# ConvFFN input product of a hybrid decoder: pairs of weight tiles multiplied by seven block products

## Chip, cores and metric

One core of a Trainium2 chip runs the whole program. The metric is the device time of one execution in microseconds (us). A profile of one execution is read beside the times.

## What is computed

Two layers of a decoder trunk run for 512 prompt tokens and 8 sample tokens, all in fp32. The part that matters is the last third of a layer, the ConvFFN, with d_model 1024 and d_ff 2816:

```python
def conv_ffn(h, buf, p):
    a, g = split_cols(h @ p['w_ffn_in'], (D_FF, D_FF))
    a, new_buf = causal_dwconv(a, buf, p['ffn_conv_w'], p['ffn_conv_b'])   # 3 taps along tokens
    return (jax.nn.silu(a) * g) @ p['w_ffn_out'], new_buf
# in decoder_layer, for each of the 2 layers
f, new_buf_ffn = conv_ffn(rmsnorm(x, p['norm_ffn_pre']), buf_ffn, p)
x = x + rmsnorm(f, p['norm_ffn_post'])
```

## The kernel before

Activations lie with features on the 128 partitions and tokens along the free dimension: a tile is `[128, 2, 260]`, two halves of 256 prompt and 4 sample tokens. A model vector is 8 such tiles (the k blocks), the hidden vector of the ConvFFN 22 (`NFF`). The kernel is written in a framework that puts each engine's instructions in an order of its own, by readiness and program order, with all semaphores; each engine then runs its queue in that order. Buffers come from pools: `ck` (56 buffers of a tile's size, function `C`), `ld` (8 buffers for loads, `LD`), weights (`wr` raw with 3 buffers, `wh` and `wl` with 4 each), PSUM (`PD` of two banks, twice; `PS` of one bank, four times).

A product keeps fp32 accuracy in one of two ways. In most, weights and activations are cut into a high part in fp32r (`wh`, a ScalarE cast, line 169) and a low part (`wl`, a VectorE subtraction, line 111), and three matmuls per k block are summed: high by high, high by low, low by high (`mm3`, line 195). `dense` does this for one 128-column tile of weights: 8 k blocks, 3 products, 2 halves. Directly after a norm, where the activations are late, `after_norm` instead multiplies uncut fp32 tiles ("exact products" below, line 407; the profile shows two matmul records for each), while `late`, a generator, finishes the residual sum, its square sums (`Sum`, `Rms`) and the cuts `sp` of x in between. In both cases 1/rms (`r`) is applied to the result when it leaves PSUM.

The ConvFFN's first product has 22 pairs of tiles, an `a` tile `wf[j]` and a gate tile `wf[NFF + j]`. The first three tiles (a 0, gate 0, a 1) are exact products in `after_norm`, the other 41 are `dense`. `ffn_a` scales the a tile by 1/rms into `pb` and calls `ffn_conv` (three taps, tanh: one ScalarE step, two VectorE steps at line 114, tanh on ScalarE, one VectorE step); `ffn_g` scales the gate tile into `gg`, `ffn_mul` multiplies on VectorE. `ffn_sample` does the sample tokens for 6 to 8 tiles at once. The results `us` are cut into `uss` (8 of them inside the loop) for the second product, `w_ffn_out`, done by `post`, whose steps alternate with the next layer's `memory_kv`. Weight loads go through SP's queue, small loads and stores through GpSimd's. GpSimd has two small instructions per pair (a memset, line 1489; a copy, line 1503). Elsewhere it multiplies whole tiles: in the mixer at lines 1142 and 296, and near the program's end in `bulk` at lines 335 and 338. VectorE's helpers are `tt` (line 111, two tensors) and `stt` (line 114, two tensors and a scalar).

## Time and profile before

| what | value |
|---|---|
| median of 3 runs | 3201.56 us (3200.24 to 3203.86) |
| profiled execution, its own time | 3205.31 us |
| its span, first to last instruction | 3203.5 us |
| mean granted TensorE clock | 0.996 |
| matmul records | 25878 |

In the rows, PE is TensorE's matmul, PEld its weight load, DVE VectorE, ACT ScalarE, POOL GpSimd, SP the engine that issues most loads. L195 is line 195. Times are from the span's start. `out<-in` names the tiles; xN counts instructions; a bracket is the idle time before and what ended it. Instructions of an engine overlap a little in the records, so the distance between two starts is the better price of one.

### The profile page before, as it was taken

The numbers are of one execution on the slowest core, as the hardware profiler recorded it, in microseconds if no ns is written. First come the engines' busy times: TensorE is split into PE (matmuls) and PEld (weight loads), VectorE is DVE, ScalarE is ACT, GpSimd is POOL, SyncE is SP. The second block draws the span as 40 slices with busy tenths as digits, with TensorE's granted clock in tenths as the row PEclk, the third lists the DMA queues.
The fourth block names the chain that finished last, engine by engine and source line by source line (L and its number), as shares of the span: only waits on it lengthen the run. The fifth ranks groups of instructions, "written<-read, shape, count | busy, mean of one in ns | idle before, by whom it ended". The sixth has DMA issues, their size and how long they took to land. (4 is left out here: it accounts for less than half of the span.)

```text
span 3203.5 us, 64089 instructions
## 1 busy us (share of the span) xinstructions
PE 3160.6 (99%) x25878; PEld 3020.2 (94%) x25878; DVE 1949.0 (61%) x3773; ACT 1454.4 (45%) x3348; POOL 423.9 (13%) x762
## 2 busy tenths in 40 slices
PE   8999999999999999999999999999999999999998
PEld 7989999999999879999999899999999998899998
DVE  6665686777553537665286666777775436376643
ACT  5343566666433434333243445676673233433331
POOL 1100222122300101000020011222223001010001
PEclk9999999999999999999999999999999999999999
DMA  7322444444643553223263234444455336432231
GB/s 258 122 83 100 140 166 150 146 162 160 215 139 107 186 172 127 96 96 109 88 228 110 80 103 162 158 140 160 153 183 197 123 109 213 147 129 96 94 96 64
DMA packets 192168, 445.83 MB, mean 139 GB/s; under 512 B 26416, under 2 KB 78656, under 8 KB 191872
## 3 DMA queue, kind: packets, MB, share of 16 engines
q1 hardware_dynamic: 162736, 353.63, 33.0%
q0 software_dynamic: 27840, 86.01, 7.9%
q8 instruction: 203, 3.33, 0.4%
q10 hardware_dynamic: 1296, 2.11, 0.2%
q14 instruction: 93, 0.76, 0.1%
HBM read 377.81 MB, written 63.83 MB: 138 GB/s over the span
## 5 line engine op out<-in xcount | busy, mean ns | idle before, releaser
L169 ACT CAST wh<-wr 128x1024 fp32r<-128x1024 f32 (+1 forms) x484 | 503.4, 1041 | 1139.6 <-PE pd L195 763.9
L111 DVE TENSOR_TENSOR wl<-wr,wh 128x1024 fp32r<-128x1024 f32 (+1 forms) x484 | 591.4, 1223 | 523.3 <-ACT wh L169 514.4
L195 PE MATMUL pd<-xih,wh 128*128 128x260 f32 x3488 | 716.8, 287 | 3.2 <-ACT dd L108 3.2
L195 PE MATMUL pd<-xih,wl 128*128 128x260 f32 x3488 | 702.6, 283 | 0.0
L195 PE MATMUL pd<-xil,wh 128*128 128x260 f32 x3488 | 702.1, 283 | 0.0
L195 PEld LDWEIGHTS pd<-xih,wh 128*128 128x128 f32 x3488 | 536.8, 189 | 25.3 <-issue 19.2
L195 PEld LDWEIGHTS pd<-xih,wl 128*128 128x128 f32 x3488 | 537.7, 188 | 0.1
L195 PEld LDWEIGHTS pd<-xil,wh 128*128 128x128 f32 x3488 | 537.6, 189 | 0.1
L195 PE MATMUL pd<-sph,wh 128*128 128x260 f32 x1472 | 298.0, 284 | 0.0
L195 PE MATMUL pd<-spl,wh 128*128 128x260 f32 x1472 | 296.4, 283 | 0.0
L195 PE MATMUL pd<-sph,wl 128*128 128x260 f32 x1472 | 295.8, 282 | 0.0
L195 PEld LDWEIGHTS pd<-sph,wh 128*128 128x128 f32 x1472 | 226.8, 188 | 2.9 <-issue 2.7
L195 PEld LDWEIGHTS pd<-spl,wh 128*128 128x128 f32 x1472 | 227.9, 189 | 0.0
L195 PEld LDWEIGHTS pd<-sph,wl 128*128 128x128 f32 x1472 | 226.7, 188 | 0.1
L114 DVE SCALAR_TENSOR_TENSOR cv<-pb,hw,cv 128x512 f32<-128x512 f32 x192 | 143.6, 748 | 5.5 <-ACT cv L108 0.7
L251 POOL TENSOR_TENSOR ny<-nms,mhalf 128x3 f32<-128x3 f32 (+2 forms) x26 | 39.2, 1506 | 787.6 <-DVE nms L250 787.6
L195 PE MATMUL pd<-uh,wh 128*128 128x260 f32 x616 | 124.1, 283 | 0.0
L195 PE MATMUL pd<-uh,wl 128*128 128x260 f32 x616 | 123.9, 282 | 0.0
L195 PE MATMUL pd<-ul,wh 128*128 128x260 f32 x616 | 123.6, 282 | 0.0
L108 ACT ACTIVATE th<-cv 128x512 f32<-128x512 f32 x64 | 40.5, 633 | 154.4 <-DVE cv L114 133.0
L296 DVE TENSOR_TENSOR acc<-acc,sq 128x260 f32<-128x260 f32 (+1 forms) x126 | 61.8, 513 | 76.6 <-ACT sq L108 75.2
L195 PEld LDWEIGHTS pd<-ul,wh 128*128 128x128 f32 x616 | 95.1, 188 | 0.0
(425 smaller groups left out, 6052.1 us busy)
## 6 DMA issues: line engine op xcount, KB each, us to landing
wr<-in_w_in SPq DMA_DIRECT2D x218, 512.0 KB
wr<-in_w_ffn_in SPq DMA_DIRECT2D x88, 512.0 KB
hs<-in_ssm SPq DMA_DIRECT2D x64, 256.0 KB
csb<-csd SPq DMA_DIRECT2D x64, 256.0 KB
out_s_ssm<-hs POOLq DMA_DIRECT2D x64, 256.0 KB, 2.8
mem_k<-in_mem_k SPq DMA_DIRECT2D x64, 256.0 KB
wr<-in_w_ssm_out SPq DMA_DIRECT2D x32, 512.0 KB
mem_v<-in_mem_v SPq DMA_DIRECT2D x64, 256.0 KB
```

Of the source, the lines that this page charges most:

```text
L108: return A.activation(out, in_, f, **kw)
L111: return V.tensor_tensor(out=out, in0=a, in1=b, op=op)
L114: return V.scalar_tensor_tensor(out=out, in0=a, scalar=s, in1=b, op0=op0, op1=op1)
L169: A.copy(h[:, :nk], raw[:, :nk])
L195: PE.matmul(ps, a[:, k], b[:, hf], start=(first and k == 0 and i == 0), stop=(last and k == nk - 1 and i == 2))
L251: G.tensor_tensor(out=y, in0=ms, in1=mhalf[:, 0:n], op=ALU.pow)
L296: (E or V).tensor_tensor(out=AV(self.acc, h), in0=AV(self.acc, h), in1=AV(sq, h), op=ALU.add)
```

## The change

The kernel multiplies the a tile and the gate tile of a pair together, for pairs 2 to 21. The pair is taken as a 2 by 2 block matrix (two tiles by two halves of the 8 k blocks), the activations as another (two halves of k by two halves of the tokens), and the four block results come from seven block products with sums of operands and results (Strassen's form, Winograd's variant) in place of eight. The weights' sums s1, s2 and two in-place differences are made on GpSimd, and each combination (`a1`, `c1` to `c4`) is cut into high and low parts by ScalarE and VectorE (`cut`). The activations' combinations (`b11`, `b21`, `b22`, `t1` to `t4`) are made once per layer in `late_seven`, from x scaled by 1/rms and the norm's gain, so no scaling is left when a result leaves PSUM. Partial results are copied from PSUM (`p`, `q`) and added to later ones. Pairs 0 and 1, four tiles, are exact products in `after_norm4`. The product with the gate moves from VectorE to GpSimd, the small sample copies to ScalarE, all cuts of `us` and the start of the next `memory_kv` behind the loop. The pool `ld` is merged into `ck` (64 buffers).

```diff
...
 PAST = 2048
 THETA = 500000.0
 NEG = -1e30
-NCK = 56
+NCK = 64
 NM1 = 18
-NLD = 8
...
         ckpool = es.enter_context(tc.tile_pool(name="ck", bufs=NCK))
-        ldpool = es.enter_context(tc.tile_pool(name="ld", bufs=NLD))
...
         def LD(s, shape, dt=F32):
-            return ldpool.tile(list(shape), dt, tag="ld", name=nm(s))
+            return ckpool.tile(list(shape), dt, tag="ck", name=nm(s))
...
-        def post(w, xs_, gain, src, keep, nwin, nxt=None, final=False):
+        def post(w, xs_, gain, src, keep, nwin, nxt=None, final=False, seven=False):
...
             r2 = C("r2") if nxt else None
-            sp = [(C("sph", dt=F32R), C("spl", dt=F32R)) for _ in range(8)] if nxt else None
+            if seven:
+                sp = {}
+            else:
+                sp = [(C("sph", dt=F32R), C("spl", dt=F32R)) for _ in range(8)] if nxt else None
...
+            def late_seven():
+                squares(0)
+                rm[1].spread(r)
+                bulk(1)
+                yield
+                rm2[0] = Rms(sq2.acc, D, 0)
+                squares(1)
+                yield
+                rm2[0].spread(r2)
+                yield
+                xn = [C("xn") for _ in range(8)]
+                def scaled(hf):
+                    for m in range(8):
+                        stt(xn[m][:, hf], mg[m][:, hf], nxt(m), r2[:, hf], ALU.mult, ALU.mult)
+                def pair(a, b):
+                    h, l = C("sxh", dt=F32R), C("sxl", dt=F32R)
+                    for i, v in enumerate((a, b)):
+                        split_to(h[:, i], l[:, i], v)
+                    return [(h[:, i], l[:, i]) for i in range(2)]
+                def put(na, nb, ps_):
+                    sp[na] = [v[0] for v in ps_]
+                    sp[nb] = [v[1] for v in ps_]
+                scaled(0)
+                put("b11", "b21", [pair(xn[k][:, 0], xn[k + 4][:, 0]) for k in range(4)])
+                yield
+                rm2[1] = Rms(sq2.acc, D, 1, pd=rm2[0].pd)
+                yield
+                rm2[1].spread(r2)
+                yield
+                scaled(1)
+                ta, tb = [], []
+                for k in range(4):
+                    a, b = C("ta"), C("tb")
+                    tt(a[:, 0], xn[k][:, 1], xn[k][:, 0], ALU.subtract)
+                    tt(a[:, 1], xn[k + 4][:, 1], a[:, 0], ALU.subtract)
+                    G.tensor_tensor(out=b[:, 0], in0=xn[k + 4][:, 1], in1=xn[k][:, 1], op=ALU.subtract)
+                    G.tensor_tensor(out=b[:, 1], in0=xn[k + 4][:, 0], in1=a[:, 1], op=ALU.subtract)
+                    ta.append(a)
+                    tb.append(b)
+                put("t1", "t2", [pair(a[:, 0], a[:, 1]) for a in ta])
+                v = [pair(xn[k + 4][:, 1], xn[k + 5][:, 1]) for k in (0, 2)]
+                sp["b22"] = v[0] + v[1]
+                put("t3", "t4", [pair(b[:, 0], b[:, 1]) for b in tb])
+                store()
+                yield
...
             if nxt:
-                return mg, sp, r2, late()
+                return mg, sp, r2, late_seven() if seven else late()
...
+        def after_norm4(aps, x, gain, late, evac):
+            steps = ((1, 2), (1, 7), (2, 4), (3, 1), (4, 4), (5, 1))
+            ws = [load_wg(ap, 8, gain) for ap in aps]
+            out = {}
+            pd = None
+            for j in range(8):
+                hf, i = divmod(j, 4)
+                if j in (4, 5):
+                    pd = pd or PD()
+                    ps = pd[:, j % 2]
+                else:
+                    ps = PS()
+                for k in range(8):
+                    PE.matmul(ps[:, :HALF], ws[i][:, k], x[k][:, hf], start=(k == 0), stop=(k == 7))
+                    if (j, k) in steps:
+                        next(late)
+                    if (j, k) in ((2, 4), (5, 1)):
+                        for i2 in range(4):
+                            if (i2, 0 if j == 2 else 1) in out:
+                                evac(i2, out.pop((i2, 0 if j == 2 else 1)), 0 if j == 2 else 1)
+                out[i, hf] = ps
+                if j == 3:
+                    for i2 in range(4):
+                        if (i2, 0) in out:
+                            evac(i2, out.pop((i2, 0)), 0)
+                if j == 5:
+                    next(late)
+            for (i2, hf), ps in out.items():
+                evac(i2, ps, hf)
+        def seven_products(ap0, ap1, X):
+            w0, w1 = [wpool.tile([P, 8, P], F32, tag="wr", name=nm("wr"), bufs=3) for _ in range(2)]
+            nc.sync.dma_start(out=w0, in_=ap0)
+            nc.sync.dma_start(out=w1, in_=ap1)
+            def W():
+                return [wpool.tile([P, 8, P], F32R, tag=t, name=nm(t)) for t in ("wh", "wl")]
+            def cut(t, x, o, n):
+                h, l = [v[:, o:o + n] for v in t]
+                A.copy(h, x)
+                tt(l, x, h.bitcast(F32), ALU.subtract)
+                return h, l
+            def sub(out, a, b, op=ALU.subtract):
+                G.tensor_tensor(out=out, in0=a, in1=b, op=op)
+            s1, s2 = C("s1", (P, 4, P)), C("s2", (P, 4, P))
+            sub(s1, w1[:, 0:4], w1[:, 4:8], ALU.add)
+            sub(s2, s1, w0[:, 0:4])
+            t = W()
+            a1 = cut(t, w0, 0, 8)
+            sub(w0[:, 4:8], w0[:, 4:8], s2)
+            sub(w1[:, 0:4], w0[:, 0:4], w1[:, 0:4])
+            t12 = W()
+            c1 = cut(t12, s1, 0, 4)
+            c2 = cut(t12, s2, 4, 4)
+            c4 = cut(W(), w0[:, 4:8], 0, 4)
+            c3 = cut(W(), w1, 0, 8)
+            def mm(ps, w, k0, xs, first):
+                h, l = w
+                for k in range(4):
+                    xh, xl = xs[k]
+                    for i, (a, b) in enumerate(((h, xh), (h, xl), (l, xh))):
+                        PE.matmul(ps, a[:, k0 + k], b, start=(first and k == 0 and i == 0), stop=(k == 3 and i == 2),
+                                  skip_group_check=True)
+            pd = PD()
+            de, be = pd[:, 0, :HALF], pd[:, 1, :HALF]
+            al, ga = PS()[:, :HALF], PS()[:, :HALF]
+            p, q = C("pp"), C("pq")
+            mm(be, a1, 0, X["b11"], True)
+            A.copy(p[:, 0], be)
+            mm(al, a1, 4, X["b21"], True)
+            yield 0, 0, al, p[:, 0]
+            mm(de, c1, 0, X["t1"], True)
+            A.copy(q[:, 0], de)
+            mm(be, c2, 0, X["t2"], False)
+            A.copy(p[:, 1], be)
+            mm(de, c4, 0, X["b22"], False)
+            yield 0, 1, de, p[:, 1]
+            mm(be, c3, 0, X["t3"], False)
+            A.copy(q[:, 1], be)
+            yield 1, 1, be, q[:, 0]
+            mm(ga, c3, 4, X["t4"], True)
+            yield 1, 0, ga, q[:, 1]
...
             x, xss, r, late = drain(post(I["w_xo"][L], oxs, lambda m: pc("xpost", m), x_src, keep, 3,
-                                         lambda m: pc("ffnpre", m)))
+                                         lambda m: pc("ffnpre", m), seven=True))
...
                 tt(QV(gth[j], hf), PV(r, hf), PV(ps, hf), ALU.mult)
                 tt(S8(g_s[:, j], hf), SV(r, hf), SV(ps, hf), ALU.mult)
-                if hf is None and j > 1:
-                    ffn_mul(j)
             def ffn_mul(j):
                 tt(PV(us[j]), PV(us[j]), QV(gth[j]), ALU.mult)
...
             wf = I["w_ffn_in"][L]
             def first(i, ps, hf):
-                (ffn_a, ffn_g, ffn_a)[i]((0, 0, 1)[i], ps, hf)
-            after_norm([wf[0], wf[NFF], wf[1]], x, lambda k: pc("ffnpre", k), late, first)
-            for j in range(1, NFF):
-                if j > 1:
-                    ffn_a(j, dense(wf[j], xss), None)
-                ps = dense(wf[NFF + j], xss)
-                ffn_g(j, ps, None)
-                if j == 1:
-                    for i in range(2):
-                        ffn_conv(i)
-                        ffn_mul(i)
+                (ffn_a, ffn_g)[i % 2](i // 2, ps, hf)
+            after_norm4([wf[0], wf[NFF], wf[1], wf[NFF + 1]], x, lambda k: pc("ffnpre", k), late, first)
+            for j in range(2):
+                ffn_conv(j)
+                ffn_mul(j)
+            for j in range(2, NFF):
+                pb = apb[j] = C("pb", (P, 520))
+                gg = C("gg")
+                G.memset(pb[:, 0:2], 0.0)
+                for i, hf, ps, part in seven_products(wf[j], wf[NFF + j], xss):
+                    if i == 0:
+                        o = 2 + 256 * hf
+                        tt(pb[:, o:o + HALF], ps, part, ALU.add)
+                        A.copy(fnew[:, j, 4 * hf:4 * hf + 4], pb[:, o + 256:o + HALF])
+                        if hf:
+                            ffn_conv(j)
+                    else:
+                        tt(gg[:, hf], ps, part, ALU.add)
+                A.copy(S8(g_s[:, j]), SV(gg))
+                G.tensor_tensor(out=PV(us[j]), in0=PV(us[j]), in1=PV(gg), op=ALU.mult)
                 if j == 8:
                     ffn_sample(0, 8)
-                if 9 <= j < 17:
-                    uss[j - 9] = split(us[j - 9], "u")
                 if j == 16:
                     ffn_sample(8, 16)
-                if j == 18 and L < DEPTH - 1:
-                    mem_dram = mem_scratch()
-                    mkv = memory_kv(L + 1, *mem_dram)
-                    next(mkv)
             ffn_sample(16, 22)
-            for j in range(8, NFF):
+            for j in range(NFF):
                 uss[j] = split(us[j], "u")
+            if L < DEPTH - 1:
+                mem_dram = mem_scratch()
+                mkv = memory_kv(L + 1, *mem_dram)
+                next(mkv)
             G.dma_start(out=O["p_ffn_conv"][L], in_=psf)
             G.dma_start(out=O["s_ffn_conv"][L, :, :, 1], in_=fnew)
             last = L == DEPTH - 1
```

## Rows read from the trace of the kernel before

**Rows 1.** The page, busy time by engine: us, share of the span, instructions.

```profile
PE 3160.6 (99%) x25878; PEld 3020.2 (94%) x25878; DVE 1949.0 (61%) x3773; ACT 1454.4 (45%) x3348; POOL 423.9 (13%) x762
```

**Rows 2.** Busy time by stretch: from:to, length, engines in turn, granted clock, DMA.

```profile
1210.00:1237.10 27.10, 25.56 (x133) 21.70 (x132) 22.18 (x55) 15.19 (x32) 9.23 (x13) 1.00 0.44 143
1237.10:1472.90 235.80, 235.80 (x1970) 235.76 (x1969) 156.63 (x280) 82.65 (x109) 9.19 (x44) 1.00 0.32 106
1472.90:1596.00 123.10, 123.10 (x1028) 123.10 (x1027) 39.59 (x54) 37.65 (x53) 1.64 (x1) 1.00 0.30 91
2823.90:3059.50 235.60, 235.60 (x1965) 235.60 (x1965) 151.39 (x269) 77.25 (x96) 9.19 (x44) 1.00 0.30 101
```

**Rows 3.** The chain that ended last, in order of time: start, us, what.

```profile
2823.89 346.66 PE pd L195 x2892
```

**Rows 4.** Groups by line in 1237.1:1472.9, TensorE: count | busy us, mean ns | idle.

```profile
L195 PE MATMUL pd<-sph,wh 128*128 128x260 f32 x656 | 132.0, 283 | 0.0
```

**Rows 5.** Timeline of VectorE in the first product: start, duration, what.

```profile
1301.46 0.69 DVE L111 TENSOR_TENSOR u<-u,gg 128x512 f32<-128x512 f32 x1
1302.07 1.22 DVE L111 TENSOR_TENSOR wl<-wr,wh 128x1024 fp32r<-128x1024 f32 x1
...
1307.37 1.22 DVE L111 TENSOR_TENSOR wl<-wr,wh 128x1024 fp32r<-128x1024 f32 x1
1308.51 0.74 DVE L114 SCALAR_TENSOR_TENSOR u<-pb,hf,u 128x512 f32<-128x512 f32 x1
1309.17 0.22 DVE L111 TENSOR_TENSOR cg<-fnew,hf 128x64 f32<-128x64 f32 x1
```

**Rows 6.** Timeline of VectorE near the program's end, 260 columns.

```profile
3184.53 4.33 DVE L335 TENSOR_TENSOR mg<-mg,r 128x260 f32<-128x260 f32 x6 [2.39 <-ACT r L277]
3188.78 0.76 DVE L338 TENSOR_TENSOR yo<-mg,xo 128x260 f32<-128x260 f32 x2
3189.46 0.42 DVE L296 TENSOR_TENSOR acc<-acc,sq 128x260 f32<-128x260 f32 x1
```

**Rows 7.** Timeline of VectorE in the mixer, at three places.

```profile
419.39 2.28 DVE L111 TENSOR_TENSOR wl<-wr,wh 128x1024 fp32r<-128x1024 f32 x1
...
474.97 0.69 DVE L114 SCALAR_TENSOR_TENSOR zt<-zt,pd 128x520 f32<-128x520 f32 x1 [0.98 <-ACT zt L108]
...
2406.89 1.75 DVE L114 SCALAR_TENSOR_TENSOR hs<-hs,dsm,ot 128x512 f32<-128x512 f32 x1
2408.57 1.77 DVE L111 TENSOR_TENSOR yal<-ld,yah 128x520 fp32r<-128x520 f32 x1
```

**Rows 8.** Timeline of GpSimd at the same places and near the end.

```profile
419.30 1.28 POOL L1142 TENSOR_TENSOR yz<-yz,zt 128x512 f32<-128x512 f32 x1 [0.95 <-DVE zt L114]
...
474.53 1.31 POOL L296 TENSOR_TENSOR acc<-acc,sq 128x520 f32<-128x520 f32 x1 [2.48 <-ACT sq L108]
...
2406.80 2.99 POOL L1142 TENSOR_TENSOR yz<-yz,zt 128x512 f32<-128x512 f32 x2 [0.83 <-DVE yz L114]
...
3184.57 1.89 POOL L335 TENSOR_TENSOR mg<-mg,r 128x260 f32<-128x260 f32 x2 [1.47 <-ACT r L277]
3186.42 1.81 POOL L338 TENSOR_TENSOR yo<-mg,xo 128x260 f32<-128x260 f32 x2
```

**Rows 9.** Groups by line in 1237.1:1472.9, VectorE (columns as in rows 4).

```profile
L114 DVE SCALAR_TENSOR_TENSOR u<-th,u 128x512 f32<-128x512 f32 x22 | 15.2, 691 | 12.2 <-ACT th L108 12.2
...
L111 DVE TENSOR_TENSOR ul<-u,uh 128x520 fp32r<-128x520 f32 x8 | 5.6, 700 | 0.0
```

**Rows 10.** Timeline of ScalarE as the stage begins.

```profile
1233.40 1.05 ACT L169 CAST wh<-wr 128x1024 fp32r<-128x1024 f32 x1 [1.03 <-issue]
...
1234.98 0.35 ACT L277 COPY r<-pd 128x260 f32<-128x260 f32 x1
```

**Rows 11.** Timeline of TensorE in the exact products.

```profile
1217.10 9.45 PE L407 MATMUL ps<-mg,wg 128*128 128x260 f32 x42
```

**Rows 12.** The page, DMA issues: what, queue, count, size, us to landing.

```profile
ld<-gd POOLq DMA_DIRECT2D x48, 260.0 KB, 4.2
```

## The prediction

> **What bounds the kernel now.** I read first the busy table of the page: TensorE is busy 3160.6 of 3203.5 us [rows 1]. An average says little about one stage, so next the busy times by stretch. The reader is to see that in both stretches of the ConvFFN's first product (1237.1 to 1472.9 and 2823.9 to 3059.5 us) TensorE is never idle, at full granted clock, while VectorE is busy 156.63 and 151.39 us, ScalarE 82.65 and 77.25, and GpSimd 9.19 of some 235.7 us [rows 2]. The chain that ended last runs through the second of these stretches as one piece of matmuls [rows 3]. So this stage is paid by the matmul, and any matmul fewer is a gain as long as the other engines keep pace. Whether they do is the whole question, so the rest was read from VectorE's and GpSimd's own rows.
>
> **Price of a matmul.** Three groups of 656 (one of them in [rows 4]) make 1968 matmuls in 235.8 us: 0.1198 us each. A tile pair now takes 96 (two tiles, 8 k blocks, 3 high/low products, 2 halves), 11.50 us.
>
> **Part 1, seven products.** Each is 4 k blocks by 3, 12 matmuls of the same 260 columns: 84, 10.06 us. That removes 12 x 0.1198 = 1.44 us per pair, 57.5 us over the 40 pairs of both layers, if TensorE stays without a pause.
>
> **Part 2, what VectorE does per pair.** Prices are distances between starts of instructions that follow each other at once [rows 5]: the low half of 1024 columns 1.14 us (1307.37 to 1308.51), a 512 column product 0.61 (1301.46 to 1302.07), a convolution step 0.66 (1308.51 to 1309.17). Of 260 columns, two take 0.68 (3188.78 to 3189.46), 0.34 each [rows 6]. New: five low halves instead of two (w0 and c3 with 1024, c1, c2, c4 with 512 columns): 2 x 1.14 + 3 x 0.61 = 4.11. Unchanged: two convolution steps and the gate, 2 x 0.66 + 0.61 = 1.93, and about 0.2 for the sample rows (an estimate from instructions like the 0.22 us one, some eight for eight tiles). These 6.24 us all read both inputs from SBUF. The four sums out of PSUM read one input there: 4 x 0.34 = 1.36. VectorE alone would thus need 7.6 us, less than 10.06.
>
> **Part 3, what GpSimd does per pair, and what it costs VectorE.** It gets s1, s2, the two in-place differences of the weights, and the product with the gate, taken from VectorE: five products of 128x512. Alone one takes 1.28 us [rows 8], 6.4 us per pair, which also looks free. But rows from elsewhere show the two engines in each other's way. A VectorE low half that begins 0.09 us after such a GpSimd instruction takes 2.28 us, not 1.22 [rows 5, 7, 8]. At 2406.8 two of GpSimd and two of VectorE take turns: VectorE 1.75 and 1.77 instead of the 0.74 and 0.69 that the same sizes take in [rows 5], GpSimd 2.99 for its two [rows 7, 8]. So one costs VectorE 1.01 to 1.08 us; I take 1.05. The exception is in the same rows: at 474.97 a VectorE instruction with one input in PSUM takes 0.69 us though GpSimd works until 475.84. A short form agrees: from 3184.5 six VectorE products of 260 columns take 4.33 us instead of 6 x 0.34 + 0.08 = 2.12 beside four of GpSimd, 0.55 for each [rows 6, 8].
>
> The two engines then share one resource: 6.24 + 5 x 1.05 = 11.5 us per pair, already all of the 11.50 of today and more than TensorE's 10.06. That is the lower end, with all 1.36 us of PSUM sums under GpSimd's instructions. With none there it is 12.85; VectorE's wait for the tanh, 12.2 us for 22 tiles today [rows 9], adds up to 0.55: 13.4. As the PSUM sums stand between two-input instructions in VectorE's queue, and GpSimd uses part of the tanh's wait, I take the middle, 12.4: +0.90 per pair, **+36 us** for 40 (ends 0 and +76). TensorE then waits for low halves in VectorE's queue. The gate's product and the four weight sums are one queue on GpSimd, so what is late there is the next pair's c1 to c4.
>
> [...]
>
> **Part 4, ScalarE and the PSUM banks.** Its 82.65 us of today [rows 2] are 4.0 per pair, with two casts of 1024; three casts of half that size, under 1.05 each, and four copies out of PSUM at 0.35 [rows 10] make at most 8.6. Nothing while the pair takes 12.4. Two banks are written again one product (1.44 us) after the product that is copied from them; a cast of 1.05 ahead of a copy of 0.35 just fits. If VectorE did not set the pace this would cost up to 0.2 us per pair, 8 in all.
>
> **Part 5, the start of each layer's stage.** The second gate tile moves into the exact products: 32 instructions at 9.45 / 42 = 0.225 [rows 11] are 7.2 us in place of 5.75: +1.45 per layer, **+3**. Scaling first and cutting combinations: 16 products, 8 differences and 28 low halves of 260 columns, 52 x 0.34 = 17.7 on VectorE, less the eight of 520 that go (5.6, as eight others of that size [rows 9]), 12.1 more; GpSimd's 8 differences hold it 8 x 0.55 = 4.4. Of 16.5 us, 4.9 fit in VectorE's idle time of that stretch (27.1 - 22.18 [rows 2]), 7.2 under the longer exact products: about 5 stay per layer, **+10** (0 to +18, as the last operand is needed only six products later).
>
> **Part 6, the end and the rest.** The 22 cuts of the result all come after the loop, 22 x 0.70 = 15.4 us of VectorE against 22 x 6 x 0.1198 = 15.8 us of matmuls that use them one by one; eight were inside before [rows 9]. They run under the second product, where VectorE is busy 39.59 of 123.1 us [rows 2]; the first few are in the open, about 2 per layer, **+4** (0 to +8). The next layer's memory preparation goes under the same stretch: nothing; without that cover, the few us that it has on VectorE. Merging the load pools gives other stages' loads other buffers: I take nothing, and all of TensorE's idle time, 42.9 us [rows 1], bounds what better loading could give.
>
> **Sum.** 36 + 3 + 10 + 4 = +53. The profiled execution took 3205.31 us (its span 3203.5); it lies 3.75 above the median of the runs, 3201.56, so I predict 3201.56 + 53 = 3255. Its own range is +3 (3204) to 76 + 3 + 18 + 8 = +105 (3306).
>
> **Rivals.** *Matmuls still set the end.* If GpSimd's instructions fall where VectorE is idle or reads PSUM, a pair takes 10.06 us: -57.5 + 3 + 4 to 10, about 3153. For it: VectorE is idle a third of the stretch today. Against it: 11.5 us of shared work don't go into 10.06. It decides below a pair of 11.1 us (11.5 less 17 / 40), which means 0.97 us or less per GpSimd instruction with all PSUM sums hidden, 0.70 with none. Chance 0.17.
>
> *The exclusion holds for the whole instruction.* Then each costs 1.28 [rows 8], 0.23 more, 1.15 per pair: 46 us more, 3301. Against: the 1.05. Chance 0.10.
>
> *The loads' chain sets the pace.* There are three raw buffers for two loads per pair, so the next w1 is loaded when c4 is cut; then s1, s2 and the two differences follow in turn. A load of half this size lands after 4.2 us [rows 12]; four sums taking turns with VectorE 4 x 1.5 = 6.0 [rows 8]; cast and cut 0.6 + 0.61 + 1.05: 12.5, with the gate's product in between 14.0 per pair: (14.0 - 11.50) x 40 + 17 = +117, 3319. For it: every step waits for the one ahead. Against: load and gate's product can overlap. Chance 0.13.
>
> *Nothing changes:* a pair of about 11.1 us. Chance 0.05.
>
> **The numbers.** The forecast's own chance is 0.55. Less than 0.2% (6.4 us) can't be told from no change by measuring this kernel. Faster 0.17, same 0.05, slower 0.55 + 0.10 + 0.13 = 0.78. From 3190 to 3330 lie the forecast, the whole-instruction case, no change and half of the loads' chain; what is left out is most of the faster case and the far end of the chain, 0.2.
>
> **What would show it.** Matmul records fall by 40 x 12 + 2 x (48 - 32) = 512. Right: pairs follow each other every 12.4 us, the 1024 column low half has a mean well over 1.22 us, GpSimd's products well over 1.28, and TensorE waits for VectorE. Wrong: pairs every 10.06 us without pauses (first rival), GpSimd idle before s1 waiting for a load (third), or pauses at the PSUM banks waiting for ScalarE (part 4). A gap of over 9 us at the stage's start would break part 5.

## The result, and the profile after

The changed kernel takes 3455.1 us (four runs, 3446.7 to 3462.0), the kernel before 3202.7 beside it (3200.2 to 3205.8): 1.0789 times as long, 95% interval 1.0776 to 1.0801. The sign was right; +53 us were forecast and +252 came, outside the range.

The page, busy time by engine and the granted clock in 40 slices:

```profile
PE 3249.8 (94%) x25366; PEld 3062.3 (89%) x25366; DVE 2179.1 (63%) x3943; ACT 1593.9 (46%) x3802; POOL 749.5 (22%) x978
...
PEclk9999999999999987888999999999999999888899
```

The 512 matmuls are gone (25878 in [rows 1]), yet TensorE is idle 210 us instead of 43, and in two places its clock is down. Busy time by stretch (from:to, length, engines in turn, granted clock): the first pair of tiles by seven products, the other 19 of the layer.

```profile
1241.10:1272.70 31.60, 15.71 (x87) 14.56 (x86) 26.82 (x53) 12.71 (x30) 10.51 (x13) 0.68 0.11 34
1272.70:1595.20 322.50, 257.94 (x1598) 237.85 (x1596) 225.01 (x262) 128.90 (x274) 153.24 (x133) 0.83 0.20 64
```

In [rows 2] TensorE was busy without a pause at full clock. Now it is idle for a fifth of the 322.5 us, and the others for longer: VectorE is busy 225 us, GpSimd 153. No engine is full, so none of them is the bound by its work. That points to a loop of waits, in which each pair waits for something of the pair before. How long one turn is, the copy into `psf` tells, which comes once per pair (count, shortest/median/longest ns, first to last start):

```profile
L1648 POOL COPY psf<-pb x10: 184/184/185, 1303.7 to 1457.2; 128x2 f32<-128x2 f32 x10
```

(1457.2 - 1303.7) / 9 = 17.06 us per pair, against 11.50 before. Over 38 steady pairs that is 211 us; the two first pairs add 2 x (31.6 - 11.5) = 40. Together 251, about the whole loss; in the trace the second product of the first layer begins at 1595.2 in place of 1472.9.

The chain that ended last, one turn of it in the second layer (start, us, what):

```profile
3135.93 0.44 DVE pb L109
...
3137.34 1.14 DVE u L112
...
3138.50 1.69 DVE u L112
...
3140.22 0.64 ACT th L106
...
3140.89 0.99 DVE u L112
3141.88 1.85 DVE wl L109 x2
...
3146.19 1.14 DVE wl L109
...
3147.96 2.62 PE pd L537 x12
...
3150.60 0.38 ACT pp L551
...
3153.11 0.44 DVE pb L109
```

It runs in a circle: pb's second sum, then the convolution of this pair (ScalarE's scale, two operations, tanh, one more: 5.95 us from the start of pb's sum), and behind these in VectorE's queue the low parts of the next pair's c1 and c2 and then of its other cuts, its products, and its pb. GpSimd's queue closes a second circle beside it. Its timeline (start, us, what, idle before):

```profile
1440.15 0.18 POOL L1648 COPY psf<-pb 128x2 f32<-128x2 f32 x1 [8.87 <-DVE pb L109]
...
1440.33 1.29 POOL L517 TENSOR_TENSOR s<-wr 128x512 f32<-128x512 f32 x1
...
1457.25 0.18 POOL L1648 COPY psf<-pb 128x2 f32<-128x2 f32 x1 [8.86 <-DVE pb L109]
```

A copy of two columns stands ahead of s1 of the next pair and waits for pb: GpSimd is idle 8.9 of 17.1 us. s1 takes nothing from that copy, and from 1438 to 1440 us no load is under way (0 DMA packets), yet s1 begins at 1440.33, as the copy ends: it stood behind it in GpSimd's queue.

TensorE's waits in the layer's stage (waiting for, us in total, times, longest):

```profile
PE pd L537 <- ACT pp L545: 39.3, 20, 4.5
PE pd L537 <- DVE wl L109: 26.4, 18, 12.7
```

The largest, 2 us per pair, is for ScalarE's copy of `be` (line 545), which stands in ScalarE's queue behind casts of the next operands:

```profile
1444.44 0.60 ACT L512 CAST wh<-s 128x512 fp32r<-128x512 f32 x1
...
1445.05 0.61 ACT L512 CAST wh<-s 128x512 fp32r<-128x512 f32 x1
1445.57 0.36 ACT L545 COPY pp<-pd 128x260 f32<-128x260 f32 x1
```

### The profile page after: what moved, and what is told of

It reads as the page before. It is cut to its first block, busy times and chain, and to the rows that moved or that the text cites. A ratio compares the mean times of both kernels' runs of the same rounds, so it can differ in the third digit from the quotient of the medians.

```text
span 3460.2 us, 64064 instructions
## 1 busy us (share of the span) xinstructions
PE 3249.8 (94%) x25366; PEld 3062.3 (89%) x25366; DVE 2179.1 (63%) x3943; ACT 1593.9 (46%) x3802; POOL 749.5 (22%) x978
## 5 line engine op out<-in xcount | busy, mean ns | idle before, releaser
L167 ACT CAST wh<-wr 128x1024 fp32r<-128x1024 f32 (+1 forms) x402 | 417.1, 1039 | 903.6 <-PE pd L193 614.8
L537 PE MATMUL pd<-sxh,wh 128*128 128x260 f32 x800 | 271.7, 340 | 81.4 <-ACT pp L545 79.3
L537 PE MATMUL pd<-sxh,wl 128*128 128x260 f32 x800 | 250.9, 321 | 52.7 <-DVE wl L109 52.7
L537 PEld LDWEIGHTS pd<-sxh,wh 128*128 128x128 f32 x800 | 180.4, 225 | 105.7 <-ACT pp L545 87.7
L537 PE MATMUL pd<-sxl,wh 128*128 128x260 f32 x800 | 255.9, 320 | 0.0
L537 PEld LDWEIGHTS pd<-sxh,wl 128*128 128x128 f32 x800 | 176.0, 223 | 60.3 <-DVE wl L109 60.2
L537 PEld LDWEIGHTS pd<-sxl,wh 128*128 128x128 f32 x800 | 182.6, 228 | 0.1
L112 DVE SCALAR_TENSOR_TENSOR u<-pb,hf,u 128x512 f32<-128x512 f32 x88 | 117.1, 1331 | 34.6 <-ACT u L106 33.3
L109 DVE TENSOR_TENSOR wl<-s,wh 128x512 fp32r<-128x512 f32 x80 | 129.6, 1656 | 0.0
L537 PE MATMUL ps<-sxh,wl 128*128 128x260 f32 x320 | 103.4, 323 | 24.7 <-DVE wl L109 24.4
```

The costliest lines, as they stand in the source:

```text
L109: return V.tensor_tensor(out=out, in0=a, in1=b, op=op)
L112: return V.scalar_tensor_tensor(out=out, in0=a, scalar=s, in1=b, op0=op0, op1=op1)
L167: A.copy(h[:, :nk], raw[:, :nk])
L537: PE.matmul(ps, a[:, k0 + k], b, start=(first and k == 0 and i == 0), stop=(k == 3 and i == 2), skip_group_check=True)
```

## The experiments

Behind each run's time stands its ratio to the kernel before, timed on the same chip, with the 95% interval. The time per pair is always taken from the starts of the copy into `psf`, as above.

**1. e1_psf_off_pool: the small copy taken off GpSimd.**

```diff
-                G.tensor_copy(psf[:, j], pb[:, 512:514])
+                A.copy(psf[:, j], pb[:, 512:514])
...
-                G.memset(pb[:, 0:2], 0.0)
+                V.memset(pb[:, 0:2], 0.0)
```

> Edit: of each of the 40 pairs, the copy of the last two columns of pb into psf goes from GpSimd to ScalarE and the memset of pb's first two columns from GpSimd to VectorE; the five weight-tile and gate products stay on GpSimd. In GpSimd's order the first instruction behind s1 of a pair that belongs to the pair before it is then the product u x gg, between s1 and s2, and it waits for the last block product of the pair before. Theory Q (a serial loop: GpSimd's sums of the next pair stand in its queue behind something that waits for this pair's products): only s1 is freed, s2 and all behind it wait still, so the steady pair stays at 16.5 to 18.5 us and the kernel at 3430 to 3510 us. Rival P (that copy alone is the trouble, 8.9 us of waiting per pair): the pair falls to about 14 us, the kernel to 3320 to 3360. Rival X (VectorE and GpSimd exclude each other, and the five products are simply too dear): unchanged within 1%, 3430 to 3480 us, with GpSimd waiting no less for VectorE.

Measured: 3505.2 us, 1.0946 (1.093 to 1.0962), 18.09 us per pair. One turn of its chain:

```profile
3265.99 0.11 POOL u L1707
...
3267.78 1.29 POOL s L517
3269.07 2.90 POOL wr L517 x2
...
3273.37 3.11 DMA wr<-in_w_ffn_in
...
3276.54 1.28 POOL s L517
3277.82 6.48 issue
```

The next thing in the queue took the copy's place: s1 is done early, then u x gg of the pair before waits for 6.5 us and holds up s2. As theory Q said, and worse than before.

**2. e1b_pool_late and e4_prepare_ahead: written in another order.** In e1b u x gg is written one pair later; in e4 the loads, sums and cuts of the next pair are written ahead of this pair's products.

```diff
-                G.tensor_tensor(out=PV(us[j]), in0=PV(us[j]), in1=PV(gg), op=ALU.mult)
+                if j > 2:
+                    G.tensor_tensor(out=PV(us[j - 1]), in0=PV(us[j - 1]), in1=PV(gprev), op=ALU.mult)
```

> Edit: as the run before, and u x gg of a pair is written one pair later, so that nothing in GpSimd's queue ahead of a weight sum waits for a product of the pair that TensorE has under way. All five 128x512 products per pair stay on GpSimd. Theory Q: the serial loop is open; what is left is the loop of the loads through the three raw buffers, 1.29 + 1.74 + 1.62 + 1.74 + 1.74 = 8.1 us of GpSimd, about 1.9 for the cast and the low part that free the buffer, 3.1 for the load and about 0.5 to issue it: a steady pair of 13 to 14 us, and the kernel at 3290 to 3360 us; TensorE's half-clock matmuls become fewer where its pauses go. Theory X (the five products with their exclusion cost the time wherever they stand): 16.5 us or more per pair, 3430 us or more.

```diff
             for j in range(2, NFF):
+                if j + 1 < NFF:
+                    cuts[j + 1] = prepare(wf[j + 1], wf[NFF + j + 1])
...
-                for i, hf, ps, part in seven_products(wf[j], wf[NFF + j], xss):
+                for i, hf, ps, part in seven_products(cuts.pop(j), xss):
```

> Edit: order alone. The weight loads, sums and cuts of pair j+1 are written ahead of the products of pair j; every instruction stays on its engine, the copy into psf and u x gg on GpSimd too. Theory Q: GpSimd still waits for a product of the pair under way, but what stands behind that wait is needed a pair later, so the pair falls to the loop of the loads, 12.5 to 14 us, and the kernel to 3260 to 3360 us. The first pair's pause of 12.97 us becomes smaller too, since its weights are cut earlier. Theory X: the same work on the same engines, 16.5 us or more per pair, 3430 us or more.

Measured: e1b 3503.9 us, 1.0943 (1.0927 to 1.0959), 17.82 us per pair; e4 3536.5, 1.1039 (1.1021 to 1.1058), 18.80. Both missed. In e1b the edit did not do what it was for: queues are filled by a scheduler that goes by its own estimate of when things are ready, and it put u x gg between s1 and s2 as in e1. In e4 the pauses moved to the copies of the accumulators (3.4 us in one pair) and to low parts (2.8). So far only one thing was shown: that order matters can't be tested by writing lines elsewhere.

**3. e3_eight_products: the rest of the change alone.** x is scaled up front, the pools are merged, the cuts of u stand behind the loop, but each pair has eight products.

> Edit: everything of the change but the seven products: x is scaled and split up front, the first two pairs go through the new routine, the load pools are merged, the splits of u stand behind the loop, the additions out of PSUM are plain copies; each pair is 96 matmuls with whole weight tiles cut as before. No weight sums on GpSimd; u x gg stays there. If the rest of the change costs what the prediction put on it (part 5 without the sums' lateness, 1.5 to 5 us per layer, and part 6, 2 per layer), the kernel takes 3205 to 3220 us; if part of the 250 us comes from the rest (merged pools, late scaling, the splits behind the loop), it takes over 3250 us. Theory Q and X both say 3205 to 3225 us.

Measured: 3213.7 us, 1.0039 (1.0024 to 1.0054), 11.51 us per pair. The rest costs 12 us, the products 241. Part of the 12 is the second product, which starts before its operands are cut. First and last start of its matmuls on the high halves, e3 and then the kernel before:

```profile
L193 PE MATMUL pd<-uh,wh x308: 278/282/420, 1468.2 to 1583.5; 128*128 128x260 f32 x154
```

```profile
L195 PE MATMUL pd<-uh,wh x308: 277/283/366, 1472.9 to 1584.6; 128*128 128x260 f32 x154
```

115.3 us in place of 111.7: 3.6 in this layer.

**4. f1, f2, f3: VectorE's circle.** f1 queues the convolution of a pair behind the next pair's sums and cuts; f2 does the same with sums and u x gg on VectorE; f3 leaves most of the convolution out.

```diff
+                with ExitStack() as es2:
+                    if j + 1 < NFF:
+                        cuts, behind = prepare(wf[j + 1], wf[NFF + j + 1])
+                        for ins in behind:
+                            es2.enter_context(tc.issue_after(ins))
+                    ffn_conv(j)
```

> Edit: order alone. The loads, sums and cuts of pair j+1 are written ahead of the convolution of pair j, and the convolution (ScalarE's scale and tanh, VectorE's three operations), the copy into psf, the copy into g_s and u x gg of pair j are queued, on each engine, behind the sums and the cuts c1, c2 and c4 of pair j+1. Every instruction stays on its engine, all five 128x512 products per pair on GpSimd. Theory S (a serial loop in VectorE's and GpSimd's order: pb's second sum, ScalarE's scale, two operations on u, tanh, the third operation, and only behind these the low parts of the next pair's c1 and c2): the loop is open, and the pair falls to what the engines' work allows, 11.0 to 13.0 us, with a kernel of 3225 to 3300 us. Theory X (the five products and their exclusion cost 17 us wherever they stand): 16 us or more per pair, 3410 us or more. Theory L (three raw buffers: load 3.1 us, sums 6.4, cut 1.9, issue 0.5, and u x gg 1.7 in between): 13.5 to 14 us, 3320 to 3340 us.

> Edit: the order of the run before, and the four weight sums and u x gg of each pair are VectorE's in place of GpSimd's, so that the two do not exclude each other in the loop. VectorE then has 6.24 + 1.36 us of the prediction's part 2 and five products of about 0.7 us, 11.1 us per pair, TensorE 10.1. Theory S: 11.1 to 12.5 us per pair, 3230 to 3285 us; beside the run before it tells what exclusion is worth once the order is open: at most 1 us per pair, 40 us in all. Theory X: this is the only one of the order runs that becomes fast, at least 100 us faster than the run before.

> Edit: the changed kernel as it is, with part of the work of 20 of 22 pairs left out: the two operations that add the neighbouring columns, the tanh and the operation behind it (four links of the chain pb, scale, two operations, tanh, operation: 1.14 + 1.69 + 0.64 + 0.99 us in the changed kernel's chain of waits). Order of the rest, loads, sums, cuts and all five products on GpSimd as in the changed kernel. Theory S: the loop loses those links, 17.1 - 4.5 = 12.6 us, so 12.5 to 14.0 us per pair if no other wait takes over, and the kernel 3280 to 3340 us. A theory in which that chain is only beside the path (GpSimd's sums behind the copy into psf, the loads, the exclusion): VectorE has slack in the pair already, so the pair stays at 15.5 us or more and the kernel at 3390 us or more.

Measured: f1 3473.3 us, 1.0852 (1.0836 to 1.0868), 17.08 per pair; f2 3576.7, 1.1178 (1.1159 to 1.1197), 19.60; f3 3446.2, 1.0767 (1.0751 to 1.0783), 16.36. Theory S fell in all three: even without the convolution the pair kept 16.4 us. In f1, TensorE waits for the casts of the next weights (waiting for, us in total, times, longest):

```profile
PE ps L543 <- ACT wh L512: 23.7, 8, 3.0
```

They now stand in ScalarE's queue behind the copy of this pair's last sum in `be`, so a third circle seems to have taken over in f1. No run opened this circle by itself, and what holds f2 at 19.60 us is not shown. The granted clock over the whole run was 0.956 to 0.958 in f1 and 0.944 to 0.946 in f2, against 0.997 and 0.998 of the kernel before. In f3 the chain of waits had gone over to GpSimd's circle. Here u x gg is followed by the last two of the next sums, a cast, the products, the sums of gg, and u x gg again:

```profile
3099.55 1.60 POOL u L1708
3101.15 2.92 POOL wr L517 x2
...
3107.26 2.60 PE pd L537 x12
...
3115.45 0.78 DVE gg L109 x2
...
3116.36 1.60 POOL u L1708
```

**5. i1_banks: tiles of their own for the accumulators.**

```diff
-            de, be = pd[:, 0, :HALF], pd[:, 1, :HALF]
-            al, ga = PS()[:, :HALF], PS()[:, :HALF]
+            al, ga = pd[:, 0, :HALF], pd[:, 1, :HALF]
+            de, be = PS()[:, :HALF], PS()[:, :HALF]
```

> Edit: the two accumulators de and be, which share one two-bank PSUM tile in the changed kernel, get a one-bank tile each, and al and ga take the two halves of the shared tile; nothing else is touched. Theory B (the tile is what waits are made for: a product into be waits for ScalarE's copy of de and the other way round, and the order of TensorE's queue, which is fixed ahead by estimated times, is bent around these waits, so that the last weight tile cut, c3, is asked for early in the pair): TensorE's 79 us of waits for the copies of the shared tile go, its queue runs through the products in the order in which they are written, and the pair falls from 17.1 to 12.5 to 14 us, the kernel to 3270 to 3340 us; the stretches of half clock go with the pauses. Theories that put the time on GpSimd's queue, on the exclusion or on the loads: nothing of theirs is touched, 16 us or more per pair, 3420 us or more.

Measured: 3334.1 us, 1.0408 (1.039 to 1.0425), 13.78 us per pair: 121 us gained by giving two accumulators tiles of their own. TensorE's waits for 200 us of it:

```profile
PE ps L537 <- DVE wl L109: 22.2, 14, 1.7
PE ps L537 <- ACT wh L512: 5.8, 2, 3.1
```

The waits for copies are gone, one pause of 1.7 us or less is left in a pair (up to 3.1 us in two), and GpSimd still waits for pb, but less:

```profile
1394.08 0.19 POOL L1648 COPY psf<-pb 128x2 f32<-128x2 f32 x1 [5.35 <-DVE pb L109]
```

The queues of the other engines kept their order. What became shorter is TensorE's part, which both circles go through. The waits came with the shared tile: de and be lay in two banks all along, and with a tile each no wait for `pp` is left in the 200 us above, where the changed kernel has 39.3 us of it in the layer's stage. The two accumulators were guarded together because they were one tile.

**6. h3, h4, h1, g1: the order kept.** The loop is written out as a pipeline and every engine's queue keeps it: h3 with separate accumulators and sums on GpSimd, h4 with sums and u x gg on VectorE, h1 as h3 with the shared tile. In all three u x gg comes one pair later and the memset of pb is VectorE's. g1 is the changed kernel with TensorE's queue alone kept.

```diff
+                return lambda *a, **k: tc.keep_in_program_order(f(*a, **k))
...
+                mm(al, p_.a1, 4, X["b21"], True)
+                tt(pb[:, 2:2 + HALF], al, p[:, 0], ALU.add)
+                if n_:
+                    n_.a1 = n_.cast(n_.W(), n_.w0, 0, 8)
+                    n_.low(n_.a1)
+                    for k in (0, 1, 3, 2):
+                        n_.sums(k)
+                mm(de, p_.c1, 0, X["t1"], True)
```

> Edit: the accumulators as in the run before, and the loop over the 20 pairs written out as a pipeline whose order is kept on every engine: the loads, sums and cuts of pair j+1 stand between the products of pair j (a1 behind the second product, the four sums behind that, c1 and c2 behind the fourth, c4 behind the fifth), the convolution of pair j in its own tail, u x gg one pair later. Every instruction stays on its engine, five 128x512 products per pair on GpSimd. Theory B: with no late operand left the pair is bounded by VectorE and GpSimd together, the prediction's 11.5 to 13.4 us, taken at 12.4: 12.3 to 13.5 us, and the kernel 3235 to 3300 us; it should tell whether the prediction's part 3 sized the engines' work rightly. Theory X (exclusion is dearer than part 3 has it): 14 us or more per pair, 3330 us or more.

> Edit: as the run before, with the four weight sums and u x gg on VectorE in place of GpSimd, so nothing in the loop excludes VectorE. VectorE has about 11.1 us of work per pair, TensorE 10.1. Theory B: 11.2 to 12.2 us per pair, and the kernel 3205 to 3260 us, 30 to 60 us below the run before; at best level with the kernel before, whose pair of tiles takes 11.5 us. If it comes out below 3190 us, the seven products pay after all; if above 3280, some other late operand is left.

> Edit: the kept order of the run h3 with de and be back in one shared two-bank tile, as in the changed kernel; the five products are on GpSimd. It crosses the two things that the separate tiles and the kept order change. Theory B1 (the waits for the copies of the shared tile themselves are the cost): at least 40 us above h3's 3314, so 3350 to 3420 us. Theory B2 (the harm is in the order of the queues, which the estimated waits bend; with the order kept, GpSimd and VectorE set the pace and the waits fall beside it): within 20 us of h3, 3300 to 3335 us.

> Edit: the changed kernel with its shared tile, and TensorE's queue alone kept in the order in which the products are written (be, al, de, be, de, be, ga of one pair, then the next), where the changed kernel asks for two products of c3 and three of the next pair's a1 right behind c1. Theory B2 with TensorE's queue alone at fault: 3320 to 3360 us, as with separate tiles. Theory B1, or B2 with the queues of VectorE, ScalarE and GpSimd at fault too: no gain, 3430 to 3500 us, since the casts and low parts still come behind the convolution and the copies of the shared tile behind the casts.

Measured: h3 3313.6 us, 1.0348 (1.0333 to 1.0364), 13.01 per pair; h4 3238.0, 1.0114 (1.0098 to 1.0129), 11.15; h1 3321.3, 1.0369 (1.0354 to 1.0385), 13.13; g1 3466.2, 1.0819 (1.0801 to 1.0837), 17.07. The total of h3 missed its range (3235 to 3300) though its pair did not; its start was costed too low. B1 fell: with the order kept the shared tile costs 8 us, not 40. TensorE's queue alone is not at fault either (g1). What h3 and h4 differ in is where five products per pair run: 75.6 us, 1.9 per pair. The clock doesn't explain it: it was 0.94 in h3 (1283.26 to 1515.00 us), but 1.00 in three pairs of h1 (1366.55 to 1405.18), at the same pace. Groups of VectorE (count | busy us, mean ns), h3 and then h4:

```profile
L110 DVE TENSOR_TENSOR wl<-s,wh 128x512 fp32r<-128x512 f32 x36 | 51.7, 1435 | 2.5 <-ACT wh L110 2.5
```

```profile
L110 DVE TENSOR_TENSOR wl<-s,wh 128x512 fp32r<-128x512 f32 x36 | 24.6, 683 | 0.0
```

Without GpSimd beside it the same low part takes 0.68 instead of 1.44 us. If VectorE set the pace in both, each product on GpSimd cost it 0.69 + 1.86 / 5 = 1.06 us, an estimate that agrees with the 1.05 of part 3 (in h3 VectorE is busy 194.5 of 231.7 us). And in h4 VectorE is the bound by its work: busy 43.13 of 44.24 us in four pairs.

```profile
1290.35:1334.59 44.24, 41.21 (x339) 40.37 (x337) 43.13 (x76) 27.25 (x57) 3.53 (x4) 1.00 0.28 96
```

**7. e1c_only_sums and m2_both_branches: both circles.** e1c takes everything that waits for a product off GpSimd; m2 leaves out the convolution as well, as f3 did.

```diff
-                G.tensor_tensor(out=PV(us[j]), in0=PV(us[j]), in1=PV(gg), op=ALU.mult)
+                V.tensor_tensor(out=PV(us[j]), in0=PV(us[j]), in1=PV(gg), op=ALU.mult)
```

> Edit: the changed kernel with u x gg and the memset of pb on VectorE and the copy into psf on ScalarE, so that GpSimd holds the four weight sums of each pair and nothing that waits for a product; de and be share their tile as before, the convolution stands where it stood. The cause as it looks now: from pb's second sum of one pair two branches lead side by side to the low parts of the next pair's c1 and c2 and from there through TensorE's products back to pb: GpSimd's (copy into psf, u x gg, sums) and VectorE's (scale, two operations, tanh, operation); run e1 opened half of the first, run f3 the second alone, so neither gained. With GpSimd's branch wholly open VectorE's is left, some 2.5 to 3.5 us shorter: a pair of 13.5 to 14.6 us and a kernel of 3310 to 3370 us. If the shared tile or TensorE's order alone is the cause: 3420 us or more.

> Edit: the run before with the two operations on the neighbouring columns, the tanh and the operation behind it left out of 20 of 22 pairs, as in run f3; both branches are open, the shared tile is kept. Two branches side by side: 11.2 to 12.5 us per pair and 3230 to 3285 us, though f3, with the same work left out, was at 3446 us. If the branches are not side by side but the copies of the shared tile set the pace: within 40 us of the run before.

Measured: e1c 3332.8 us, 1.0411 (1.0397 to 1.0426), 13.91 us per pair; m2 3263.8, 1.0196 (1.018 to 1.0211), 11.71. Both as expected. Leaving the convolution out gained 9 us in f3 and 69 here. e1c also takes one of the five products off GpSimd; by h3 and h4 that is worth 75.6 / 5 = 15 us (an estimate), so most of its 122 us are waits. In e1c the chain is VectorE's circle and nothing of GpSimd's:

```profile
3015.36 0.44 DVE pb L109
...
3016.77 0.89 DVE u L112
3017.68 1.67 DVE u L112
...
3021.69 0.69 DVE wl L109
...
3026.56 1.70 PE pd L537 x12
...
3028.34 0.44 DVE pb L109
```

**8. q1_every_second: fewer pairs by seven.** VectorE's 11.15 us per pair are above TensorE's 10.06, but a pair by eight leaves VectorE time (busy 156.63 of 235.80 us in [rows 2]). So on e3, from pair 7 on, only every second pair goes by seven.

```diff
+                if j not in (7, 9, 11, 13, 15, 17, 19, 21):
+                    ps = dense(wf[j], xss["all"])
+                    ps2 = dense(wf[NFF + j], xss["all"])
+                    if j + 1 in (7, 9, 11, 13, 15, 17, 19, 21):
+                        cuts[j + 1] = prepare(wf[j + 1], wf[NFF + j + 1])
```

> Edit: on run e3 (the rest of the change with eight products), every second pair from 7 to 21, 8 of 22, by seven products, with de and be in tiles of their own, the sums and u x gg on VectorE; the block sums of x are made during the pairs 2 to 5, the cuts of a pair by seven ahead of the convolution of the pair by eight before it, and four of the splits of u in the last pairs of the loop. VectorE's work of two pairs, about 11.1 + 6.9 us, is then under TensorE's 10.1 + 11.5, so the matmuls set the end: e3's 3213.7 less 2 x 8 x 12 matmuls of 0.1198 us, 23.0 us, and 1 to 3 us for the splits: 3187 to 3196 us, 0.2 to 0.5% under the kernel before. If the pairs by seven still wait for their cuts (over 1.4 us each), 3205 us or more.

Measured: 3189.2 us, 0.9964 (0.9951 to 0.9976), 11 us under the kernel before. In the middle of the stage TensorE has no pause and the full clock again:

```profile
1300.00:1460.00 160.00, 160.00 (x1328) 159.27 (x1327) 130.07 (x229) 82.05 (x162) 11.69 (x31) 1.00 0.30 103
```

## Why the prediction was wrong

**Prices of a matmul, parts 1 and 2: right.** 512 matmuls went; in q1 192 fewer than in e3 brought 24.5 us where 23.0 were reckoned, and 1 to 3 more for the splits of u; in h4, where VectorE does all the work and is full, a pair takes 11.15 us, and part 2's 7.6 and five of 0.69 make 11.05.

**Part 3: the step that failed.** Its price of the work was about right: with the order kept, five products on GpSimd give 13.01 us per pair (12.4 taken, 11.5 to 13.4 as its ends), and 1.9 us more than on VectorE. What failed is the step from work to time: "The two engines then share one resource", from which part 3 took the work on that resource for the time of the pair. In the changed kernel neither is full. The pair takes 17.06 us because its queues make a loop: pb of one pair, then two branches side by side (GpSimd's copy, u x gg and sums; VectorE's convolution), then the next pair's low parts, products, copies and pb. Part 3 even named the place, "what is late there is the next pair's c1 to c4", but charged nothing for it. The missing term is 17.06 - 12.4 = 4.7 us per pair, 177 us over 38 pairs. Part of it is the clock, on which the prediction had no term: in the chain above twelve matmuls take 2.62 us, at a granted clock of 0.50, in e1c's 1.70, so 0.9 us per pair in that link alone. The exclusion, that is the turns which VectorE and GpSimd take in [rows 7, 8], matters in it too, but as length of a chain: the operations on u take 1.14 and 1.69 us where [rows 5] have 0.74, and h4, with the five products on VectorE, 0.75 in the mean.

That two branches stand side by side, GpSimd's the longer, explains most of the misses: f3 opened VectorE's alone and left GpSimd's (16.36 us per pair), e1 half of GpSimd's, g1 straightened one queue, and 9 us was the most that was gained, while e1c (GpSimd's whole branch, 122 us), m2 (both, 191 us), i1 (the part common to both, 121 us) and h1 (all queues, 134 us) gained. f1 is not explained by it: it queued both branches behind the next pair's cuts and lost 18 us, as far as its trace shows to the third circle.

**Part 4** allowed at most 0.2 us per pair for the PSUM banks; 2 us per pair were waited there. It looked at the bank that is written again and at one cast ahead of the copy, not at the two casts that stand there, nor at the other accumulator in the same tile.

**Part 5: mis-sized.** 6.5 us per layer were taken (with the exact tile). The first pair took 31.6 us, 14.5 more than a steady one, with VectorE busy 26.8 of them. The gap of over 9 us that was to break it was there: TensorE's wait of 12.7 us for a low part, shown above. VectorE's timeline shows the first low part of the weights, 2.28 us, behind 20 low parts of x, two of which take 0.96 us beside GpSimd's two products from 1241.34 to 1243.15 us, the others 0.42:

```profile
1241.59 3.88 DVE L109 TENSOR_TENSOR sxl<-ta,sxh 128x260 fp32r<-128x260 f32 x8
1245.39 1.44 DVE L109 TENSOR_TENSOR sxl<-xn,sxh 128x260 fp32r<-128x260 f32 x4
1246.75 2.80 DVE L109 TENSOR_TENSOR sxl<-tb,sxh 128x260 fp32r<-128x260 f32 x8
...
1252.28 2.28 DVE L109 TENSOR_TENSOR wl<-wr,wh 128x1024 fp32r<-128x1024 f32 x1
```

It was costed by VectorE's free time, without the order in which late_seven asks for things. **Part 6** (+2 per layer) is 3.6 in e3.

**The rivals.** That a chain sets the pace was the right kind of rival, with the wrong members and too short (14.0 us). In these chains loads come onto the path once GpSimd's s1 is early: 3.11 us in e1's chain, and in e1b GpSimd is idle 5.24 us before s1, until a load lands. That the exclusion holds for the whole 1.28 us is not borne out: the 1.06 above is nearer to the 1.05 taken. Matmuls set the end only where VectorE has less to do (q1: TensorE busy 160.0 of 160 us, VectorE 130.1).

In sum, by medians: the rest of the change 12 us (e3); seven products in a kept order on VectorE 24 (h4 less e3, whose steady pair is shorter but whose first takes 27.2 us); five products on GpSimd 76 (h3 less h4); the order and the shared tile 142 (the changed kernel less h3). 254, against 252 measured; as differences along one row of runs they add up by construction. The 142 contain the clock (the last section), which was not measured by itself.

## What to carry to other kernels

When work is moved to engines that have time, cost the loop as well as the work: follow one item from its last sum to the next item's first operand through every engine's queue (here one copy that waited for pb kept GpSimd idle for 8.9 of 17.1 us), and look for two branches before undoing one. A stage in which no engine is full and the copies come at a fixed distance (here 17.06 us) points to such a loop. Give accumulators that are read at different times tiles of their own (121 us in i1), and if the helper engine is full, use the cheaper form only as often as it keeps up.

## What the hardware showed besides

In some stretches with short pauses TensorE's granted clock was lower, in others not. In the changed kernel's 322.5 us it was 0.83, moving between 1.00 (1442.0 to 1444.0 us, matmul starts 0.12 us apart) and 0.50 (1452.0 to 1454.9 us, 0.22 us apart); the longest pause of an ordinary pair was 1.6 us, and 4.5 us in the two pairs behind the sample rows. At most (1 - 0.83) x 322.5 = 55 us per layer went that way (an estimate). In i1 pairs with the same 1.7 us of idle time come at both paces, two pairs at a granted clock of 0.88 and two at 1.00:

```profile
2931.90:2959.21 27.31, 23.93 (x171) 23.45 (x169) 22.71 (x24) 13.26 (x28) 16.07 (x15) 0.88 0.24 78
3014.59:3039.74 25.15, 21.76 (x171) 20.59 (x169) 22.89 (x25) 13.38 (x28) 16.32 (x15) 1.00 0.26 84
```

1.1 us per pair, with the same work. In h1 TensorE is idle as long, 5.3 of 38.6 us in three pairs, and keeps the full clock; from 1283 to 1515 us its idle time comes in 70 waits of 0.49 us in the mean, the longest 1.5:

```profile
1366.55:1405.18 38.63, 33.29 (x254) 30.82 (x253) 29.29 (x39) 18.94 (x41) 27.13 (x18) 1.00 0.24 83
```

So pauses stand beside a lower clock in the changed kernel (0.83) and in some pairs of i1 (0.88), and beside the full clock in other pairs of i1 and in h1 (1.00); what decides it is not settled here.
